# Output weights in three steps, and the side work of the output projections and of the first FFN products as timed events with four direct operands

## The chip, the core and the metric

The kernel runs on one core of a Trainium2 chip. The metric is the device time of one execution in microseconds (us). Times of runs are medians; the profile is of one further execution, traced by the hardware. Engines are named as the profile names them: PE (matrix products, PEld its weight loads), DVE (vector), ACT (scalar and activation), POOL, and SP, which here only issues DMAs. Each engine takes its instructions in one fixed order, and an instruction waits on semaphores for results of other engines or for DMAs. So an instruction that waits holds up everything behind it on its engine.

## What is computed

One layer of an encoder for two sequences of 1024 tokens with 1024 features (a prompt and a sample, which share the weights and are independent). Cut to what matters:

```python
def encoder_layer(x, ...):
    h = rms_norm(x, norm1)
    proj = h @ w_in                      # 1024 x 1792: q, k, v, gu, gv
    ...
    a = rms_norm(windowed_gqa(q, k, v, q_gain, k_gain, sink, rel_table), attn_out_gain)
    g = rms_norm(chunked_spatial_gating(gu, gv, v_gain, w_s, b_s), gmlp_out_gain)
    x = x + jnp.concatenate([a, g], axis=-1) @ w_o          # 1024 x 1024
    h2 = rms_norm(x, norm2)
    x = x + (jax.nn.silu(h2 @ w_gate) * (h2 @ w_up)) @ w_down   # 1024 x 2816, 2816 x 1024
```

The gating mixes the 128 positions of a chunk with one 128x128 matrix for each of 8 heads, and multiplies the result with `gelu(gu)`.

## The kernel before

The 2048 tokens are 16 tiles of 128 (`t` = 0 to 15; `s` = 0, 1 is the sequence). Every product is made with operands split in a high and a low half, so that one product takes three matmuls for each 128x128 block of weights. The work runs in stages.

**Attention and projections** end near 290 us. **The gating stage** follows, to about 455 us. It is the loop `for t in range(NT)` (L815). For each tile it makes two projections, `pgv` (`gm_pieces(t, 0)`) and `pgu` (`gm_pieces(t, 1)`), 8 k steps of 3 matmuls each. After every four tiles, at t = 5, 9 and 13, and once behind the loop, `gm_group` (L670) mixes the positions: for each head 3 matmuls into a `sg` tile in one of 4 PSUM buffers (L679 to L681), and two DVE operations (L684) that take it out again, into `u`. Beside this the output weights are made ready. `wo_step(k)` (L725) loads two blocks of `w_o`, multiplies them with their gain on ACT (L731), and makes two of six operands and their differences; `wo_step2(k)` makes the other four. Each operand costs an ACT cast (L113) and a DVE subtraction (L114). `WO_AT` and `WO2_AT` say behind which tile each stands.

**The output projections** run to 636 us: eight calls of `o_pair(n)` (L883), each for two tiles, `t` and `t + 4`. The product of 2x2 blocks is made with seven block products in place of eight, in the order `wa`, `wb`, `wa` again, `wc`, `wd`, `wc` again, `wd` again; a product is 12 matmuls. Their operands are sums of blocks of the transposed mixed activations: `o_turn(n + 1)` loads the `mix` tiles from DRAM, transposes them on PE (`pm`, 16 transposes) and makes operands `mo` on ACT and DVE. It is called in pair n behind product 1. Behind products 3 and 4, `o_h2` norms the tiles of the pair before: it transposes `xs` on PE (`ph`), scales by the norm weights on ACT into `hf` (L957), and stores blocks and block sums of the hidden state to DRAM (`t_d`). `o_norm` (L874) makes `xs` from the residual: a square with its sum on ACT (L878), a small power on DVE and POOL, and a multiplication on ACT (L880). `pair_hooks` (L1241) hangs loads of the FFN's operands on the last four pairs.

**The FFN** begins at 636.5 us with `matrix(n)` (L1127): gate and up products, each again seven block products of 12 matmuls (`pa`, `pb`, `pa`, `pc`, `pd`, `pc`, `pd`; L1079 to L1081). Their left operands `top` come back from `t_d` by `top_load` (`tr`, 512 KB each) and are split by `top_conv` on ACT (L997) and DVE (L998). In matrices 0 to 3, each step takes along `prep_op` (weights of a later matrix, L121 and L122) and `top_step` (loads and splits for the sample). Copies of the products out of PSUM, `ua` (L1197) and `ub` (L1208, L1212), stand on ACT among these. The down projection ends the program.

The order on each engine is not written out by hand. A scheduler takes the code order as the priority and, by its own costs, lets later instructions go first on an engine where it expects the earlier to be waiting. Buffers come from pools with tags (`XL`, `XN`, `S`, `L`), so a load waits until the last reader of its slot is done.

Of the kernel before, what the change touches and what calls it, by code (L numbers as in the profile page):

```python
# [16 lines left out]
P = 128  # L17
# [18 lines left out]
POS = ['', 't', '', '0', '1', '']  # L36
MIX_UP = 256.0
WO2_AT = (8, 10, 12, 14)
WO_AT = (6, 8, 10, 12)
# [12 lines left out]

TW = {
# [11 lines left out]
def kernel(  # L65
# [461 lines left out]
    def gm_pieces(t, z):  # L527
        nm_ = ("gv", "gu")[z]
        if z == 0:
            pxg[t] = k4("S", f"xg{t}", (P, 2, GW))  # L530
        elif t % GROUP:
            pxg[t] = grp[t // GROUP][0][t % GROUP // 2][:, t % 2, :]
# [4 lines left out]
        if z:  # L537
            dst = pxg[t] if t % GROUP else pxg[t][:, 1]
# [244 lines left out]
    def o_turn(n):  # L783
        xts, pms = [], []
        for t in pairs[n]:
            mx_ = k4("XL", f"mix{t}")
            load(mx_[:, 0:AW], mix_a[t])
            load(mx_[:, AW:D], mix_g[t])
            for z in range(2):
# [4 lines left out]
                pms.append(pt)  # L794
        for t in pairs[n]:
            xt = k4("XN", f"xr{t}")
            load(xt, xn[t])
            xts.append(xt)
        sc = h16(f"sc{n}", (P, 8, 4, P), F32)
        a11, a12, p21, a22 = pms  # L800
        a21, s1, s2, s3, s4 = (sc[:, i] for i in range(5))
        tl = [k4("S", f"mo{n}_{i}", (P, 2, 2, 4, P), F16) for i in range(4)]
        ops = [(tl[i // 2][:, i % 2, 0], tl[i // 2][:, i % 2, 1]) for i in range(7)]
        split16(*ops[0], a11)
# [3 lines left out]
        split16(*ops[5], a22)  # L808
        nc.vector.tensor_sub(s3, a11, a21)
# [4 lines left out]
        split16(*ops[4], s1)  # L814
        split16(*ops[6], s4)  # L815
        st_b[n] = (xts, sc, ops)

    for t in range(NT):
# [4 lines left out]
        if t % GROUP:  # L823
            if t == 1:
                gm_chain(0)
            if t % GROUP != 1 or t == 1:
                gm_chain(t)
        if t > GROUP and t % GROUP == 1:
            gm_group(t // GROUP - 1)
            gm_chain(t - 1)  # L830
            gm_chain(t)
        if t == NT - 1:
            o_turn(0)
        run(gm_pieces(t, 1))
# [9 lines left out]
        if t in WO2_AT:  # L844
            wo_step2(WO2_AT.index(t))

# [27 lines left out]
    def o_norm(t, xt):  # L874
# [8 lines left out]
    def o_pair(n, hooks=()):  # L883
        (x_t, x_u), sc, ops = st_b.pop(n)
# [7 lines left out]
        def half(j):  # L892
            if n >= 1:
                o_h2(pairs[n - 1][j])

        def turn():
            if n + 1 < len(pairs):
                o_turn(n + 1)

        def extra(i):  # L900
            for fn in hooks[i] if hooks else ():
                fn()
            for c in POS[i]:
                if c == "0":
                    half(0)
                elif c == "1":
                    half(1)
                else:
                    turn()

        pa = mm(f"wa{n}", [P, 512])
        o_product(ops, 0, pa, True, True)
        nc.scalar.copy(u2, pa)
        extra(0)
        pb = mm(f"wb{n}", [P, 512])
        o_product(ops, 1, pb, True, True)
        nc.vector.tensor_add(u2, pb, u2)
        extra(1)
        o_product(ops, 2, pa, False, True)
        done(x_t, 0, pa)  # L920
        extra(2)
        pc = mm(f"wc{n}", [P, 512])
        o_product(ops, 3, pc, True, True)
        nc.scalar.copy(p7, pc)
        extra(3)
        pd = mm(f"wd_{n}", [P, 512])
        o_product(ops, 4, pd, True, True)
        nc.scalar.copy(p5, pd)
        nc.vector.tensor_add(p7, p7, u2)
        extra(4)  # L930
        o_product(ops, 5, pc, False, True)
# [4 lines left out]
        o_norm(pairs[n][1], x_u)  # L936
        extra(5)
        o_product(ops, 6, pd, False, True)
        nc.vector.tensor_add(u2, pd, u2)
        done(x_t, 1, u2)  # L940
        o_norm(pairs[n][0], x_t)

    hfs = {}

    def o_h2(t):
        s, i = divmod(t, TS)
        half, q = divmod(i, 4)
        xs = st_b.pop(("x", t))
        hf = k4("L", f"hf{t}", (P, KD, P))
        for z in range(2):  # L950
# [4 lines left out]
            for j in range(4):  # L955
                k = z * 4 + j
                nc.scalar.mul(hf[:, k, :], pt[:, j, :], n2s[:, k : k + 1])  # L957
        cs = slice(q * P, (q + 1) * P)
        if half == 0:
            hfs[t] = hf  # L960
            store(t_d[s][B11][:, :, cs], hf[:, 0:4, :])
            store(t_d[s][B21][:, :, cs], hf[:, 4:8, :])
# [3 lines left out]
        store(t_d[s][B22][:, :, cs], b22)  # L966
# [6 lines left out]
        for op, src in ((T1, ta[:, 0]), (T2, ta[:, 1]), (T3, tb[:, 0]), (T4, tb[:, 1])):  # L973
            store(t_d[s][op][:, :, cs], src)

    B11, T2, B21, T3, T1, T4, B22 = range(7)
    tops = {}
    top16 = {}
# [3 lines left out]
    def top_load(s, i, z, tag="XL"):  # L982
        traw[s, i, z] = k4(tag, f"tr{s}_{i}_{z}", (P, 2, 512))
        load(traw[s, i, z], t_d[s][i][:, 2 * z : 2 * z + 2, :])

    def top_conv(s, i, z):
        if z == 0:
            if i < 4:
                if i % 2 == 0:
                    top16[s] = h16(f"top{s}_{i}", (P, 2, 2, 4, 512), F16)  # L990
                tops[s, i] = (top16[s][:, i % 2, 0], top16[s][:, i % 2, 1])
            else:
                tops[s, i] = tuple(k4("L", f"top{s}_{i}{c}", (P, 4, 512), F16) for c in "hl")
        hi, lo = tops[s, i]
        raw = traw.pop((s, i, z))
# [78 lines left out]
    def product(key, s, i, ps, first, last):  # L1074
        op = wops[key, i]
        th, tl = tops[s, i]
        for k in range(4):
# [19 lines left out]

    tq = [(i, z) for i in range(7) for z in range(2)]
    tn = [0]

    def top_step():
        k = tn[0]
        tn[0] += 1
        if k % 2 == 0:
            if k >= 4:
                top_conv(1, *tq[k // 2 - 2])
            top_load(1, *tq[k // 2])
        elif k == 2 * len(tq) - 1:
            top_conv(1, *tq[-2])
            top_conv(1, *tq[-1])  # L1110
# [405 lines left out]
```

## Time and profile before

| | us |
|---|---|
| median of 3 runs (1853.16 to 1853.8) | 1853.62 |
| the profiled execution | 1855.08 |
| its span in the trace | 1853.3 |
| PE busy (98% of the span) | 1815.3 |
| DVE busy (63%) | 1158.5 |
| ACT busy (54%) | 1009.5 |

The mean TensorE clock granted in that execution was 0.995. Read the table from the PE row: PE runs through nearly the whole span, so the time is PE's work plus PE's waits, and the waits are few. The view of the trace that lists them, by the instruction that waited and what released it, is where the prediction starts.

### The profile page before, as it was taken

The page shows a single profiled execution, that of the slowest core. Times are in us where ns is not written, and L with a number is a line of the kernel's source. Part 1 is how long each engine was busy: PE and PEld are TensorE (multiplying, and loading weights), DVE is VectorE, ACT ScalarE, POOL GpSimd, SP SyncE. Part 2 cuts the span into 40 slices and gives each one's busy share as a digit, 9 for nine tenths or more (in the row PEclk, how much of TensorE's full clock was granted, in tenths as well). Part 3 has the DMA queues.
Part 4 walks back from the last instruction along what each step waited for, and adds up shares of the span by engine and source line. Part 5 has one row for each costly group of instructions (what it writes and reads, how often), then busy time and mean ns, then how long its engine had stood idle before and what let it go on. Part 6 is the DMA issues. An engine that isn't in the chain of part 4 may idle for free.

```text
span 1853.3 us, 26039 instructions
## 1 busy us (share of the span) xinstructions
PE 1815.3 (98%) x9696; PEld 992.3 (54%) x9696; DVE 1158.5 (63%) x2183; ACT 1009.5 (54%) x1918; POOL 106.1 (6%) x139
## 2 busy tenths in 40 slices
PE   8999999999998999999999999999999999999999
PEld 7678767878554444444444444444444444444444
DVE  4988883665777896555545645645556956555761
ACT  6899997754666775444535534534444553333340
POOL 2122110111100000000000000000000000000000
PEclk9999999999999999999999999999999999999999
DMA  7799998432667874322313313313262764333641
GB/s 243 166 190 183 194 200 268 159 103 80 209 217 252 283 244 158 125 86 109 119 69 131 108 41 120 114 63 114 86 240 101 250 199 137 103 105 101 235 139 46
DMA packets 216027, 282.05 MB, mean 152 GB/s; under 512 B 103091, under 2 KB 137907, under 8 KB 215900
## 3 DMA queue, kind: packets, MB, share of 16 engines
q1 hardware_dynamic: 215724, 280.11, 49.4%
q8 instruction: 76, 1.25, 0.3%
q10 hardware_dynamic: 144, 0.26, 0.1%
q14 instruction: 51, 0.42, 0.1%
q0 software_dynamic: 32, 0.02, 0.0%
HBM read 177.04 MB, written 80.23 MB: 139 GB/s over the span
## 4 chain that ended last, share of the span: by engine, by line
PE 61%; DVE 2%; DMA 1%; ACT 1%; issue 0%; SPq 0%; POOL 0%; DVEq 0%
PE pd L1353 7%; PE pd L1355 7%; PE pd L1354 7%; PE pd L1079 4%; PE pd L1080 4%; PE pd L1081 4%; PE pa L1079 4%; PE pc L1079 4%; PE pa L1080 4%; PE pc L1080 4%; PE pc L1081 4%; PE pa L1081 4%; PE pb L1079 2%; PE pb L1080 2%; PE pb L1081 2%; DMA tr<-t_d 1%
## 5 line engine op out<-in xcount | busy, mean ns | idle before, releaser
L1355 PE MATMUL pd<-wop,a 128*128 128x512 f16 x616 | 233.5, 379 | 0.0
L1354 PE MATMUL pd<-wop,a 128*128 128x512 f16 x616 | 233.5, 379 | 0.0
L1353 PE MATMUL pd<-wop,a 128*128 128x512 f16 x616 | 233.5, 379 | 0.0
L1080 PEld LDWEIGHTS <-op 128*128 128x128 f16 x1232 | 120.6, 98 | 149.0 <-issue 7.4
L1081 PEld LDWEIGHTS <-op 128*128 128x128 f16 x1232 | 120.5, 98 | 146.5 <-issue 1.4
L1079 PEld LDWEIGHTS <-op 128*128 128x128 f16 x1232 | 122.3, 99 | 143.1 <-issue 0.3
L1079 PE MATMUL pa<-top,op 128*128 128x512 f16 x352 | 133.4, 379 | 0.5 <-ACT ua L1197 0.5
L1081 PE MATMUL pa<-top,op 128*128 128x512 f16 x352 | 133.4, 379 | 0.0
L1080 PE MATMUL pa<-top,op 128*128 128x512 f16 x352 | 133.4, 379 | 0.0
L121 ACT ACTIVATE wop<-wd,wdr_r 128x512 f16<-128x512 f32 x66 | 47.2, 720 | 150.9 <-PE pd L1355 147.4
L121 ACT ACTIVATE a<-as,asr_r 128x512 f16<-128x512 f32 x154 | 102.1, 710 | 33.6 <-DMA as<-act_d 15.4
L122 DVE SCALAR_TENSOR_TENSOR a<-as,asr_r,a 128x512 f16<-128x512 f32 x154 | 108.7, 746 | 6.3 <-ACT a L121 6.2
L1208 ACT COPY ub<-pc 128x512 f32<-128x512 f32 x44 | 25.7, 585 | 158.9 <-PE pc L1081 158.9
L122 DVE SCALAR_TENSOR_TENSOR wop<-wd,wdr_r,wop 128x512 f16<-128x512 f32 x66 | 49.2, 749 | 98.0 <-ACT wop L121 98.0
L1353 PEld LDWEIGHTS <-a 128*128 128x128 f16 x616 | 60.4, 98 | 72.5
L1355 PEld LDWEIGHTS <-a 128*128 128x128 f16 x616 | 60.3, 98 | 72.7
L1354 PEld LDWEIGHTS <-a 128*128 128x128 f16 x616 | 60.3, 98 | 72.6
L1022 ACT ACTIVATE junk_e<-g 128x1024 f32<-128x1024 f32 x44 | 46.3, 1053 | 70.4 <-DVE g L1192 70.4
L1214 DVE TENSOR_TENSOR ub<-ub,ua 128x512 f32<-128x512 f32 x44 | 30.4, 691 | 81.6 <-ACT ub L1208 79.2
L439 ACT ACTIVATE sc<-sc,mx 128x384 f32<-128x384 f32 (+1 forms) x128 | 74.3, 582 | 10.8 <-DVE mx L423 10.6
L1189 ACT ACTIVATE g<-g,rs 128x512 f32<-128x512 f32 x57 | 41.1, 721 | 62.5 <-DVE g L1224 35.5
L1079 PE MATMUL pd<-top_6h,op 128*128 128x512 f16 x176 | 66.7, 379 | 3.9 <-ACT ub L1212 3.7
(367 smaller groups left out, 4561.9 us busy)
## 6 DMA issues: line engine op xcount, KB each, us to landing
as<-act_d SPq DMA_DIRECT2D x77, 512.0 KB, 3.6
act_d<-g SPq DMA_DIRECT2D x66, 256.0 KB, 2.0
xs<-in_xT_dram SPq DMA_DIRECT2D x28, 512.0 KB, 4.4
tr<-t_d SPq DMA_DIRECT2D x28, 512.0 KB, 5.3
raw<-in_wg_dram SPq DMA_DIRECT2D x24, 512.0 KB, 4.0
raw<-in_wu_dram SPq DMA_DIRECT2D x24, 512.0 KB, 4.2
act_d<-sa SPq DMA_DIRECT2D x44, 256.0 KB, 2.5
act_d<-sb SPq DMA_DIRECT2D x44, 256.0 KB, 3.0
```

Source lines behind the costliest of these rows:

```text
L121: nc.scalar.mul(hi, src, gain)
L122: nc.vector.scalar_tensor_tensor(lo, src, gain, hi, ALU.mult, ALU.subtract)
L439: nc.scalar.activation(sc[:, v, :W], sc[:, v, :W], AF.Exp, bias=self.mn[:, h : h + 1], scale=-1.0, accum_out=self.sums[:, h : h + 1],)
L1022: nc.scalar.activation(junk_e[0], src, AF.Square, accum_out=acc)
L1079: nc.tensor.matmul(ps, op[:, 0, k, :], th[:, k, :], start=first and k == 0, stop=False, **more)
L1080: nc.tensor.matmul(ps, op[:, 0, k, :], tl[:, k, :], start=False, stop=False, **more)
L1081: nc.tensor.matmul(ps, op[:, 1, k, :], th[:, k, :], start=False, stop=last and k == 3, **more)
L1189: nc.scalar.activation(dst, src, AF.Silu, scale=iv)
L1214: nc.vector.tensor_add(p7, p7, u2)
L1353: nc.tensor.matmul(ps, a[:, 0, s, cs], wop[:, 0], start=first and n == 0, stop=False, **kw)
L1354: nc.tensor.matmul(ps, a[:, 0, s, cs], wop[:, 1], start=False, stop=False, **kw)
L1355: nc.tensor.matmul(ps, a[:, 1, s, cs], wop[:, 0], start=False, stop=end, **kw)
```

## The change

It has four parts. Line numbers in the changed code are some 5 to 40 higher.

1. The output weights come in three steps: `wo_load` (the two loads) behind tiles 5, 7, 10 and 11, `wo_step` behind 6, 8, 11 and 12 (before: 6, 8, 10, 12), `wo_step2` behind 7, 10, 11 and 13 (before: 8, 10, 12, 14). The gain multiplications may no longer be moved ahead of code that stands before them.
2. At t = 5, 9 and 13 the heads of the group and the k steps of `pgu` stand alternately in the code.
3. `o_turn` becomes `turn_a`, `turn_b`, `turn_c`; loads of `mix` and `xr`, `o_norm`, `o_h2`, the stores (`o_put`), the loads and splits of `top` and the first weights become events with a time in a table `DT`. The unit is one product; pair n begins at 7n, matrix n at 56 + 7n. Before each product `tick` runs what is due. `top_step`, `pair_hooks` and `POS` go.
4. Four operands of the prompt (`B11`, `T2`, `B21`, `T3`, the numbers 0 to 3) are split straight from `hf`, `ta` and `tb` into their `top` tiles (16 splits of 128x4x128, an ACT cast and a DVE subtraction each). Their 16 stores `t_d0_0` to `t_d0_3`, 8 loads `tr0_0` to `tr0_3` and 8 splits of 128x1024 go.

The issues on SP fall from 736 to 712, the DVE instructions go from 2184 to 2192, those on ACT from 1588 to 1596; PE has 9696 matmuls as before.

```diff
-WO2_AT = (8, 10, 12, 14)
-WO_AT = (6, 8, 10, 12)
+WO2_AT = (7, 10, 11, 13)
+WO_LD = (5, 7, 10, 11)
+WO_AT = (6, 8, 11, 12)
...
+DT = dict(
+    mx0=-13.949, mx1=-11.679, xr0=-11.199, xr1=-7.545, ta=-5.743, tb=-3.638, tc=1.886, nu=8.268, nt=8.797, h0=10.459,
+    p0=13, h1=14.83, p1=15.401, raw0=45.957, raw1=54.748, prep=52.704, preps=0.249, tl=57.369, tls=0.412, tk=58.051,
+    tks=0.597, ul=64.811, uls=0.974, uk=67.481, uks=0.956,
+)
...
+    def wo_load(k):
+        wraw[k] = [k4("XN", f"wr{j}", (P, 2, 512)) for j in (k, k + 4)]
+        for r, j in zip(wraw[k], (k, k + 4)):
+            load(r, w_o[j * P : (j + 1) * P, :].rearrange("p (z d) -> p z d", z=2))
+
     def wo_step(k):
-        r0 = k4("XN", f"wr{k}", (P, 2, 512))
-        r1 = k4("XN", f"wr{k + 4}", (P, 2, 512))
-        wraw[k] = (r0, r1)
+        r0, r1 = wraw[k]
         for r, j in ((r0, k), (r1, k + 4)):
-            load(r, w_o[j * P : (j + 1) * P, :].rearrange("p (z d) -> p z d", z=2))
-            nc.scalar.mul(r, r, wgain[:, j : j + 1])
+            tc.keep_in_program_order(nc.scalar.mul(r, r, wgain[:, j : j + 1]))
...
+        up = gm_pieces(t, 1)
         if t > GROUP and t % GROUP == 1:
-            gm_group(t // GROUP - 1)
+            group = gm_group_pieces(t // GROUP - 1)
+            while run(group, 1):
+                run(up, 1)
             gm_chain(t - 1)
             gm_chain(t)
...
-        run(gm_pieces(t, 1))
+        run(up)
...
+    def o_put(t):
+        s, i = divmod(t, TS)
+        half, q = divmod(i, 4)
+        hf = h2s.pop(t)
+        puts.append(t)
         cs = slice(q * P, (q + 1) * P)
+
+        def put(op, src):
+            if s == 0 and op < 4:
+                if op % 2 == 0 and (s, op) not in tops:
+                    top_pair(s, op)
+                hi, lo = tops[s, op]
+                split16(hi[:, :, cs], lo[:, :, cs], src)
+            else:
+                store(t_d[s][op][:, :, cs], src)
...
+        def mul(i, ps, first, last):
+            if n < 6:
+                tick(56 + 7 * n + i)
+            product(key, s, i, ps, first, last)
...
+    def tick(time):
+        while side and side[0][0] <= time:
+            _, _, fn, args = side.pop(0)
+            fn(*args)
+
+    for n, pair in enumerate(pairs):
+        T = 7 * n
+        for j, t in enumerate(pair):
+            if n:
+                do(T + DT[f"mx{j}"], mix_load, t)
+                do(T + DT[f"xr{j}"], xr_load, t)
+            do(T + DT["nt" if j == 0 else "nu"], o_norm, t)
+            do(T + DT[f"h{j}"], o_h2, t)
+            do(T + DT[f"p{j}"], o_put, t)
+        if n:
+            do(T + DT["ta"], turn_a, n)
+            do(T + DT["tb"], turn_b, n)
+            do(T + DT["tc"], turn_c, n)
+    do(DT["raw0"], load_raw, (0, 0), "S")
+    do(DT["raw1"], load_raw, (0, 1))
+    for i in range(7):
+        do(DT["prep"] + i * DT["preps"], prep_op, (0, 0), i)
+    for k in range(6):
+        do(DT["tl"] + k * DT["tls"], top_load, 0, 4 + k // 2, k % 2)
+        do(DT["tk"] + k * DT["tks"], top_conv, 0, 4 + k // 2, k % 2)
+    for k in range(14):
+        do(DT["ul"] + k * DT["uls"], top_load, 1, k // 2, k % 2)
+        do(DT["uk"] + k * DT["uks"], top_conv, 1, k // 2, k % 2)
+    side.sort(key=lambda e: e[:2])
     for n in range(len(pairs)):
-        o_pair(n, pair_hooks(n))
...
+        o_pair(n)
+    tick(56)
```

How this moves instructions is seen at three places. The first is DVE at t = 9, ahead of the first two operations that take `sg` out (`wo..l` are low halves of output weight operands, `wr` raw output weights, `xl` the low half of a later tile's input). Before:

```order
L114 TENSOR_TENSOR wo0l<-wr_5438,wo0h 128x512
L735 TENSOR_TENSOR wr_5438<-wr_5438 128x512
L114 TENSOR_TENSOR wo4l<-wr_5438,wo4h 128x512
L736 TENSOR_TENSOR wr_5438<-wr_5439,wr_5438 128x512
L114 TENSOR_TENSOR wo2l<-wr_5439,wo2h 128x512
L737 TENSOR_TENSOR wr_5439<-wr_5439,wr_5438 128x512
L114 TENSOR_TENSOR wo3l<-wr_5438,wo3h 128x512
L684 SCALAR_TENSOR_TENSOR u_0_4858<-sg_0_5220,cst,u_0_4858 128x2x64
L684 SCALAR_TENSOR_TENSOR u_1_4859<-sg_0_5220,cst,u_1_4859 128x2x64
L684 SCALAR_TENSOR_TENSOR u_0_4858<-sg_1_5226,cst,u_0_4858 128x2x64
```

After:

```order
L196 TENSOR_TENSOR xl_5191<-xs_5187,xh_5189 128x1024
L119 TENSOR_TENSOR wo1l<-wr_5112,wo1h 128x512
L119 TENSOR_TENSOR wo5l<-wr_5112,wo5h 128x512
L688 SCALAR_TENSOR_TENSOR u_0_4883<-sg_0_5220,cst,u_0_4883 128x2x64
L688 SCALAR_TENSOR_TENSOR u_1_4884<-sg_0_5220,cst,u_1_4884 128x2x64
L688 SCALAR_TENSOR_TENSOR u_0_4883<-sg_1_5230,cst,u_0_4883 128x2x64
L688 SCALAR_TENSOR_TENSOR u_1_4884<-sg_1_5230,cst,u_1_4884 128x2x64
L688 SCALAR_TENSOR_TENSOR u_0_4883<-sg_2_5239,cst,u_0_4883 128x2x64
L688 SCALAR_TENSOR_TENSOR u_1_4884<-sg_2_5239,cst,u_1_4884 128x2x64
```

Of the third pair of weight blocks, seven operations stood right ahead of the first `u<-sg`; now none of that pair does, and the last weight operations there are of the pair before it, behind which `xl` also stands. On PE, behind each `sg` (3 matmuls) there are now 3 matmuls of `pgu`. At t = 13, the order after has seven operations of the last two weight blocks ahead of the first `u<-sg` of that group, where before there were two `xl` and two `vl`.

The second place is SP in the output projections, at the loads of `mix10` and `mix14`, which PE transposes for pair 6 (`x1_d` are stores of the residual, `tr0` loads of FFN operands, `xr` loads of the residual). Before:

```order
L875 DMA x1_d12_138<-xr12_6778 128x1024
L984 DMA tr0_1_0_7191<-t_d0_1_143 128x1024
L875 DMA x1_d8_134<-xr8_6776 128x1024
L797 DMA xr13_7001<-in_xn_dram 128x1024
L787 DMA mix10_7207<-mix_a10_104 128x512
L788 DMA mix10_7207<-mix_g10_120 128x512
L787 DMA mix14_7220<-mix_a14_108 128x512
L788 DMA mix14_7220<-mix_g14_124 128x512
L797 DMA xr10_7233<-in_xn_dram 128x1024
L984 DMA tr0_1_1_7290<-t_d0_1_143 128x1024
```

After:

```order
L793 DMA mix10_6930<-mix_a10_104 128x512
L798 DMA xr7_6460<-in_xn_dram 128x1024
L794 DMA mix10_6930<-mix_g10_120 128x512
L798 DMA xr8_6596<-in_xn_dram 128x1024
L911 DMA x1_d7_133<-xr7_6460 128x1024
L911 DMA x1_d3_129<-xr3_6367 128x1024
L991 DMA t_d0_6_148<-hf6_6933 512x1x128
L991 DMA t_d0_4_146<-ta6_7008 512x1x128
L793 DMA mix14_7047<-mix_a14_108 128x512
L794 DMA mix14_7047<-mix_g14_124 128x512
L991 DMA t_d0_5_147<-tb6_7009 512x1x128
```

The loads of `mix10` and `mix14` stood behind the stores of tiles 12 and 8, the residual of pair 4, with `tr0` loads on both sides; now `mix10` stands ahead of, and `mix14` behind, the stores of tiles 7 and 3, the residual of pair 3, and no `tr0` load is near.

The third place is ACT in matrix 2 of the FFN (names `.._1_0_0`), ahead of the copy `ua1_0_0`, for which PE's third product of that matrix waits (`junk_e` are squares with their sum; `tr1` loaded operands of the sample). Before:

```order
L121 ACTIVATE op1_0_6_8209<-st1_0_8147,es_er_5997 128x512
L997 CAST top1_2_8190<-tr1_3_0_8193 128x1024
L1022 ACTIVATE junk_e_8214,asum0_6101<-g0_0_1_7931 128x1024
L997 CAST top1_2_8190<-tr1_3_1_8254 128x1024
L1022 ACTIVATE junk_e_8214,asum0_6101<-g0_0_0_7930 128x1024
L1197 COPY ua1_0_0_8232<-pa1_0_0_8234 128x512
```

After:

```order
L1036 CAST top1_0_8143<-tr1_1_0_8124 128x1024
L1036 CAST top1_0_8143<-tr1_1_1_8146 128x1024
L1061 ACTIVATE junk_e_8187,asum0_6101<-g0_0_1_7786 128x1024
L1036 CAST top1_2_8247<-tr1_2_0_8166 128x1024
L1061 ACTIVATE junk_e_8187,asum0_6101<-g0_0_0_7785 128x1024
L1226 COPY ua1_0_0_8205<-pa1_0_0_8207 128x512
```

The copy still stands behind the square of `g0_0_0`, but the splits ahead of it are of the operands 1 and 2 now, where they were of operand 3. On PE, between `pb1_0_0` and that third product, 7 of the 12 matmuls of `pc1_0_0` stand now; before, all 12 did.

More of the change, by code (lines that the diff above doesn't have):

```diff
@@ L808, in o_turn, with turn_b @@
         split16(*ops[5], a22)
+        st_b[n][2].extend((0, 2, 5))
+    def turn_b(n):
+        sc, ops, done = st_b[n]
+        a11, a12, p21, a22 = pms.pop(n)
+        a21, s1, s2, s3, s4 = (sc[:, i] for i in range(5))
         nc.vector.tensor_sub(s3, a11, a21)
@@ L832 @@
         if t == NT - 1:
-            o_turn(0)
-        run(gm_pieces(t, 1))
+            for q in pairs[0]:
+                mix_load(q)
+            turn_a(0)
+            for q in pairs[0]:
+                xr_load(q)
+            turn_b(0)
+            turn_c(0)
+        run(up)
         if 1 <= t < 5:
@@ L881, in o_norm, with o_pair, product @@
         st_b["x", t] = xs
-    def o_pair(n, hooks=()):
-        (x_t, x_u), sc, ops = st_b.pop(n)
+    def o_pair(n):
+        def product(i, ps, first, last):
+            tick(7 * n + i)
+            assert i in st_b[n][2]
+            o_product(st_b[n][1], i, ps, first, last)
+        sc = st_b[n][0]
+        x_t, x_u = (xrs.pop(t) for t in pairs[n])
         flat = [sc[:, i].rearrange("p a b -> p (a b)") for i in range(8)]
@@ L935, in o_pair @@
         done(x_u, 1, p7)
[L936 to L938 removed]
+        x1s[pairs[n][1]] = x_u
+        product(6, pd, False, True)
         nc.vector.tensor_add(u2, pd, u2)
         done(x_t, 1, u2)
[L941 to L943 removed]
+        x1s[pairs[n][0]] = x_t
+        del st_b[n]
+    x1s = {}
+    hfs, h2s, puts = {}, {}, []
     def o_h2(t):
[L946 to L947 removed]
         xs = st_b.pop(("x", t))
@@ L983, in top_load, with top_pair @@
         traw[s, i, z] = k4(tag, f"tr{s}_{i}_{z}", (P, 2, 512))
+        assert s == 0 or len(puts) == NT
         load(traw[s, i, z], t_d[s][i][:, 2 * z : 2 * z + 2, :])
+    def top_pair(s, i):
+        pair = h16(f"top{s}_{i}", (P, 2, 2, 4, 512), F16)
+        for j in range(2):
+            tops[s, i + j] = (pair[:, j, 0], pair[:, j, 1])
     def top_conv(s, i, z):
@@ L1147, in prep @@
                     soon((1, 0), i)
-                top_step()
                 return
```

164 lines of the change are left out of this document (54 added, 110 removed).

## The prediction

> **What bounds the kernel now.** I read the busy shares first.
>
> ```profile
> PE 1815.3 (98%) x9696; PEld 992.3 (54%) x9696; DVE 1158.5 (63%) x2183; ACT 1009.5 (54%) x1918; POOL 106.1 (6%) x139
> ```
>
> PE is busy for 98% of the span and the number of matmuls stays, so a change can win only PE's idle time and slow matmuls, and lose only by new waits of PE. The second view, PE's waits, lists most of that idle time (line, releaser, total, times, longest).
>
> ```profile
> PE sg L679 <- DVE u L684: 5.4, 3, 4.5
> PE pm L793 <- DMA mix<-mix_a: 4.3, 2, 2.2
> PE pd L1079 <- ACT ub L1212: 3.7, 2, 1.9
> PE ph L954 <- ACT xs L880: 2.3, 1, 2.3
> PE wa L870 <- ACT sc L913: 1.1, 2, 0.7
> PE pd L1080 <- DVE top_6l L998: 0.9, 1, 0.9
> PE pa L1079 <- ACT ua L1197: 0.5, 1, 0.5
> PE pc L1079 <- ACT ub L1208: 0.4, 1, 0.4
> PE pd L1079 <- ACT top_6h L997: 0.2, 1, 0.2
> ```
>
> All nine lie in code that the change touches, and they sum to 18.8 us. The waits of the attention stage, which it leaves alone, are not quoted. The third view, the span in windows (wall time, busy time and instructions of PE, PEld, DVE, ACT and POOL, then the granted clock, the share of the DMA engines and GB/s), says where they lie.
>
> ```profile
> 350.00:400.00 50.00, 45.52 (x201) 38.08 (x200) 36.15 (x76) 35.04 (x63) 6.56 (x8) 0.93 0.44 149
> 400.00:450.00 50.00, 50.00 (x242) 42.10 (x241) 17.93 (x47) 18.48 (x40) 4.39 (x8) 1.00 0.22 74
> 550.00:600.00 50.00, 45.50 (x244) 24.57 (x242) 36.58 (x59) 33.76 (x73) 4.00 (x5) 1.00 0.77 249
> 600.00:650.00 50.00, 46.78 (x234) 24.73 (x235) 40.01 (x62) 40.05 (x90) 3.65 (x5) 0.97 0.87 280
> 650.00:700.00 50.00, 46.14 (x211) 20.51 (x210) 45.49 (x63) 35.65 (x51) 0.00 (x0) 1.00 0.76 245
> ```
>
> The first row holds the group at t = 9, the second tiles behind it without any PE idle, the next two the last output projections and matrix 0, the last the next matrices. In two rows the granted clock is below 1. Asked in windows that fit the dips, PE alone:
>
> ```profile
> 374.70:381.50 6.80, 5.81 (x20) 0.50 0.25 77
> 641.00:644.40 3.40, 1.11 (x9) 1.00 0.95 354
> 644.40:647.80 3.40, 3.40 (x15) 0.50 0.75 235
> 579.86:586.66 6.80, 6.80 (x45) 1.00 0.85 308
> ```
>
> After the waits at 375 and 643 us PE ran at half clock: 5.81 us busy at 0.50 did 2.9 us of work, so 2.9 us were lost, and 3.40 / 2 = 1.7 us at the second. After the wait of 2.2 us for `mix`, which ends where the last window begins, it did not. So what hangs on these waits is 18.8 + 2.9 + 1.7 = 23.4 us.
>
> The Trainium skill, "TensorE: Matmul & The Clock Gate", section "HAM oscillation — how this bites in real kernels", gives as the rule that PE should have no idle gap above about 3.4 us. By that rule the 2.3 us wait would have cost its own length only and the sum would be 1.7 us smaller; the row of 0.50 behind it says otherwise, so the measurement decides, and a short new wait may carry a dip.
>
> **Part by part.** *Weights and heads at t = 9.* The operations of DVE ahead of the wait, and the matmul that waited:
>
> ```profile
> 368.92 0.69 DVE L114 TENSOR_TENSOR wo0l<-wr,wo0h 128x512 f16<-128x512 f32 x1 [1.93 <-ACT wo0h L113]
> ...
> 374.94 2.15 DVE L684 SCALAR_TENSOR_TENSOR u<-sg,cst,u 128x128 f32<-128x128 f32 x8
> ```
> ```profile
> 375.69 0.55 PE L679 MATMUL sg<-vh,ws_hi 128*128 128x256 f32 x1 [4.48 <-DVE u L684]
> ```
>
> Seven operations of output weights, with waits for ACT among them, filled DVE from 368.9 to 375 us; four `sg` filled the four buffers and the fifth had to wait. In the order after, none of these seven is ahead of the `u` operations, so the 4.48 us and the 2.9 us of half clock go: -7.4. The two matters cover each other: even if DVE came late, three matmuls of `pgu` now lie behind each `sg`. A product of 12 such matmuls takes 2.59 us (rows below), so that is 0.65 us for each of the four heads, 2.6 us in all. The weight work itself does not vanish: it moves to t = 10 to 13, where the row of 400 to 450 us leaves DVE and ACT busy less than 19 of 50 us, and to t = 13, where seven operations now stand ahead of `u`. The same delay there, less 2.6 us, would cost 1.9 us; nothing at the other end, if ACT's casts come earlier. I take 0.5, near nothing, since by the code order the last weights' loads stand two tiles ahead. The 0.9 us of the last group (5.4 - 4.48) stays: its order is as before.
>
> *Output projections.* The waits for `mix` (4.3) and for `wa` (1.1) sum to 5.4 us. Both `mix` loads of each pair are now issued a pair earlier, on SP ahead of what held them, so -4.3. The copy out of `wa` moves up ACT's order, ahead of the squares: -1.1. The steady pair is the cover for everything else that was moved here, so it has to be walked, first PE, then ACT:
>
> ```profile
> 507.24 1.91 PE L793 MATMUL pm<-ident,mix 128*128 128x128 f32 x16
> 508.98 0.38 PE L870 MATMUL wa<-wo2h,mo 128*128 128x512 f16 x1
> ...
> 514.16 1.04 PE L954 MATMUL ph<-ident,xs 128*128 128x128 f32 x8
> 515.04 0.38 PE L870 MATMUL wd<-wo4h,mo 128*128 128x512 f16 x1
> ...
> 517.63 1.04 PE L954 MATMUL ph<-ident,xs 128*128 128x128 f32 x8
> ```
>
> ```profile
> 507.75 1.15 ACT L880 ACTIVATE xs<-xr,a_r 128x1024 f32<-128x1024 f32 x1 [0.45 <-POOL a_r L156]
> 511.81 1.66 ACT L113 CAST mo<-sc 128x512 f16<-128x512 f32 x3
> 518.31 2.18 ACT L957 ACTIVATE hf<-ph,n2s 128x128 f32<-128x128 f32 x8
> ```
>
> From start to start, a tile's `ph` takes 0.88 us, a product 2.59 (515.04 to 517.63), the `pm` of a pair 1.74. In the order after, a pair's ACT has between the first `ph` and the second `xs` product: `hf` (2.18), two squares (2.1; one of this shape takes 1.06 in a row below), two casts and a copy (1.5), `xs` (1.05), three casts (1.5, at about 0.5 each behind one another), `xs` (1.15). That is 9.5 us, from about 3.0 us after the pair's start (behind one product and half of the `ph` transposes) to 12.5. PE needs this `xs` for the next `ph` after four products, one `ph` and the `pm` transposes: 4 x 2.59 + 0.88 + 1.74 = 13.0. The slack is 0.5 us. Bounds are nothing, and 1 us in each of 6 pairs; I take 0.5 us in all, near the walked slack. The 16 splits of direct operands, 0.5 us of ACT and at most 0.69 us of DVE each, are in that walk; what they replace, splits of 128x1024, is below.
>
> *The FFN's start.* The wait of `ph` at matrix 0 goes, since the last `ph` are spread over matrix 0 and their `xs` are made earlier: -2.3 - 1.7. The waits of matrices 0 to 3 (3.7 + 0.9 + 0.5 + 0.4 + 0.2 = 5.7) are for ACT and DVE, which split what is loaded for `top`:
>
> ```profile
> 686.38 1.06 ACT L1022 ACTIVATE junk_e<-g 128x1024 f32<-128x1024 f32 x1 [3.71 <-DVE g L1192]
> 690.12 0.56 ACT L1197 COPY ua<-pa 128x512 f32<-128x512 f32 x1
> ```
> ```profile
> 683.14 1.22 DVE L998 TENSOR_TENSOR top<-tr,top 128x1024 f16<-128x1024 f32 x1
> 684.27 0.69 DVE L1221 TENSOR_TENSOR ub<-ub 128x512 f32<-128x512 f32 x1
> 684.88 0.75 DVE L122 SCALAR_TENSOR_TENSOR op<-st,es_er,op 128x512 f16<-128x512 f32 x1
> 685.54 0.75 DVE L1192 SCALAR_TENSOR_TENSOR g<-ub,es_er,g 128x512 f32<-128x512 f32 x1
> ```
> ```profile
> tr<-t_d SPq DMA_DIRECT2D x28, 512.0 KB, 5.3
> ```
>
> These change but do not all go. In matrix 0 a copy `ub` now stands behind a split: between nothing and 1.9 us, the longest `ub` wait of before; I take 0.65, since a split (1.0) and no load is ahead of it. `top_6h` keeps its 0.2. In matrix 3 the `ub` copy behind the loads of `top_6` lies between the same ends; I take 0.6, since these loads are issued earlier.
>
> Matrix 2 can be walked. There the copy `ua1_0_0` stands behind the splits of `tr1_1_1` and `tr1_2_0`, whose loads wait for a slot until DVE has split `tr1_0_0` and `tr1_0_1`. One after another DVE's operations take 1.13 us (split), 0.61 (add) and 0.66 (`op`). With the matrix's start as zero, the fifth product of matrix 1 ends at -5.2; copy (0.6), add, `op` and split give -2.2; `op`, add and split 0.2. With 5.3 us of landing the second load is there at 5.5; split (1.0), square (1.2) and copy (0.6) end at 8.2 or 8.3. PE asks after two products and 7 matmuls, at 6.7: a wait of 1.5 us. If the load takes 4 us, it is 0.4 (then DVE's result for the square comes last), if 6.5, 2.7. New and left: 0.65 + 0.2 + 0.6 + 1.5 = 2.95.
>
> **Sum.** -7.4 + 0.5 - 5.4 + 0.5 - 4.0 - 5.7 + 2.95 = -18.55 us. The profiled execution took 1855.08 us, so 1836.5; it stands 1.46 us above the median 1853.62, which gives 1835.1, say 1835.0.
>
> **Rivals.** (A) *All waits go*: -23.4 and the 0.9 of the last group back, 1831.1. For it speaks that many loads are issued earlier; against it that DVE is busy 45.5 of 50 us from 650 to 700. (B) *ACT comes late in the pairs and at matrix 2*: 1 us in six pairs (+5.5 on my 0.5), 2.7 us with a half-clock dip at matrix 2 (+1.2 + 1.7): 1843.5. For it speaks the slack of 0.5 us. (C) *The change doesn't do what it says at the weights*: the wait of t = 9 turns up at t = 13 with its half clock, 4.5 + 2.9 where I have 0.5: 1842.0. The seven operations speak for it, the `pgu` matmuls behind each `sg` against it. (D) *Slower*: the second `xs` of a pair is 2.5 us late in ACT's order, so PE waits 2.0 us and falls to half clock for a window, 1.7 us; six pairs cost 22.2 us, which is 1856.8 with 0.5 taken off. It decides from an `xs` that ends past 15 us of the pair's start instead of 12.5; against it speaks that ACT is busy 33.8 of 50 us there, and that no wait of that kind stood in pairs 1 to 5.
>
> **How the numbers follow.** My forecast has 0.55, A 0.13, B 0.15, C 0.08, B and C together, 1850.4, 0.05, D 0.04. The range reaches from A to past B, 1830 to 1845, and leaves the last two out. About 0.2% (3.7 us) is what a measurement of this kernel can tell from no change: faster by more 0.91, within 0.05, slower by more 0.04.
>
> **What would show it.** In the trace after: no `sg` wait at about 370 us and a granted clock of 1 there; no `pm` wait; in each pair no `ph` wait on `xs`, or one of under 0.5 us; at matrix 2 a `pa` wait on `ua` of 0.4 to 2.7 us; waits of about 3 us in matrices 0 to 3 in place of 5.7. Wrong would be: a `sg` wait at t = 13, `ph` waits in every pair, or a clock of 0.5 behind a wait that I have as short.

## The result and the profile after

The changed kernel takes 1835.32 us, the median of 4 runs (1832.81 to 1836.35), beside 1853.71 us before (4 runs): a ratio of 0.9888, 95% interval 0.9874 to 0.9902. The forecast was 1835.0 in a range of 1830 to 1845. The profiled execution took 1836.35 us, its span is 1834.5. First the busy shares of the changed kernel, and below them its view of PE's waits (line, releaser, total, times, longest; lines are those of the changed code):

```profile
PE 1809.8 (99%) x9696; PEld 988.6 (54%) x9696; DVE 1161.2 (63%) x2191; ACT 1005.3 (55%) x1926; POOL 104.4 (6%) x139
```
```profile
PE po L489 <- DMA pT<-ph: 6.1, 4, 3.2
...
PE pa L1119 <- ACT ua L1226: 2.0, 1, 2.0
PE pc L1119 <- ACT ub L1237: 1.5, 2, 1.0
PE sg L683 <- DVE u L688: 0.9, 2, 0.6
```

Of the nine kinds of wait that the prediction listed, with 18.8 us, these three are left in the code that was changed, with 4.4 us. No `pm`, `wa`, `ph` or `top_6` is among them, and `sg` has the 0.9 us of the last group only. (`po` is in the attention stage, which the change leaves alone; it comes up again at the end.) The same windows as before, then the one dip that is new:

```profile
350.00:400.00 50.00, 50.00 (x233) 41.78 (x233) 31.43 (x67) 29.37 (x61) 4.94 (x9) 1.00 0.43 148
550.00:600.00 50.00, 50.00 (x269) 27.16 (x267) 41.04 (x69) 35.57 (x86) 3.40 (x4) 1.00 0.64 218
600.00:650.00 50.00, 49.53 (x249) 24.84 (x248) 40.28 (x61) 40.26 (x85) 3.55 (x4) 1.00 0.72 235
650.00:700.00 50.00, 47.00 (x211) 20.80 (x209) 44.22 (x59) 31.84 (x44) 0.00 (x0) 0.97 0.75 248
668.50:671.90 3.40, 1.41 (x8) 1.00 0.87 320
671.90:675.30 3.40, 3.40 (x10) 0.50 1.00 368
```

Where PE was busy 45.5 of 50 us at t = 9 and in the last output projections, it is busy without a break. The loss that remains lies in matrices 0 to 3, and the greater part at matrix 2: a wait of 2.0 us and, behind it, 3.4 us at half clock.

The change of the profiled executions is 1855.08 - 1836.35 = 18.73 us. The terms as measured: t = 9 gave 7.4, `mix` and `wa` 5.4, `ph` at matrix 0 with its dip 4.0, and in matrices 0 to 3 5.7 went, 0.5 + 2.0 + 1.0 of waits and 1.7 of dip came. That makes 17.3. Of the other 1.4 us, the attention stage had one half clock (1.7) less and 1.2 us more of `po` wait in this execution; the rest, 0.9 us, isn't placed.

### The profile page after: what moved, and what is told of

Its sections match the earlier page's. It is cut to its first block, busy times and chain, and to the rows that moved or that the text cites. A ratio compares the mean times of both kernels' runs of the same rounds, so it can differ in the third digit from the quotient of the medians.

```text
span 1834.5 us, 26027 instructions
## 1 busy us (share of the span) xinstructions
PE 1809.8 (99%) x9696; PEld 988.6 (54%) x9696; DVE 1161.2 (63%) x2191; ACT 1005.3 (55%) x1926; POOL 104.4 (6%) x139
## 4 chain that ended last, share of the span: by engine, by line
PE 91%; DVE 3%; DMA 2%; ACT 2%; issue 1%; POOL 0%; SPq 0%; ACTq 0%; POOLq 0%; DVEq 0%
PE pd L1382 7%; PE pd L1383 7%; PE pd L1381 7%; PE pa L1119 4%; PE pa L1121 4%; PE pa L1120 4%; PE pd L1119 4%; PE pd L1121 4%; PE pd L1120 4%; PE pc L1120 4%; PE pc L1121 4%; PE pc L1119 4%; PE pb L1119 2%; PE pq L226 2%; PE pb L1120 2%; PE pb L1121 2%
## 5 line engine op out<-in xcount | busy, mean ns | idle before, releaser
L1119 PE MATMUL pc<-top_5h,op 128*128 128x512 f16 x176 | 66.7, 379 | 1.5 <-ACT ub L1237 1.5
```

The costliest lines, as they stand in the source:

```text
L1119: nc.tensor.matmul(ps, op[:, 0, k, :], th[:, k, :], start=first and k == 0, stop=False, **more)
```

## The experiments

All ratios are to runs of the kernel before on the same chip. Between chips the kernel before ran from 1853.7 to 1856.0 us, so kernels are compared by their ratio or within a set.

**Each part of the gating stage undone.** Heads ahead of `pgu` again:

```diff
-            while run(group, 1):
-                run(up, 1)
+            run(group)
```

> The changed kernel, with the heads of each group ahead of pgu again and not alternating with it; the weights stay in three steps. My theory: the seven weight operations ahead of the first u were the cause of the 4.5 us wait at t = 9, and they stay away there, so the sg wait at t = 9 is under 1 us and the clock there is 1; at t = 13, where seven operations stand ahead of u, the 2.6 us cover is gone and a wait of 1.9 to 4.5 us shows. In all 1 to 6 us above the changed kernel. Rival: the alternation is what removed the wait at t = 9; then about 4.5 us and a half clock return there, 7 us or more above the changed kernel.

Measured: ratio 0.9885 (0.9870 to 0.9900), as the changed kernel. There is no `sg` wait at t = 9, and one of 1.4 us at t = 13:

```profile
420.51 0.36 PE L683 MATMUL sg<-vh,ws_hi 128*128 128x256 f32 x1 [1.43 <-DVE u L688]
```

So the dates of the weights suffice at t = 9; at t = 13, where they put the same work, it is the alternation that hides it. The wait there was smaller than I had it, 1.4 for 1.9 to 4.5, and of the 1 to 6 us that I expected in the time nothing shows.

The weights at their old tiles, loads inside the first step, heads alternating:

```diff
-WO2_AT = (7, 10, 11, 13)
-WO_LD = (5, 7, 10, 11)
-WO_AT = (6, 8, 11, 12)
+WO2_AT = (8, 10, 12, 14)
+WO_AT = (6, 8, 10, 12)
...
-        r0, r1 = wraw[k]
+        r0 = k4("XN", f"wr{k}", (P, 2, 512))
+        r1 = k4("XN", f"wr{k + 4}", (P, 2, 512))
+        wraw[k] = (r0, r1)
         for r, j in ((r0, k), (r1, k + 4)):
-            tc.keep_in_program_order(nc.scalar.mul(r, r, wgain[:, j : j + 1]))
+            load(r, w_o[j * P : (j + 1) * P, :].rearrange("p (z d) -> p z d", z=2))
+            nc.scalar.mul(r, r, wgain[:, j : j + 1])
```

> The changed kernel, with the weights in two steps at the old tiles (loads inside the first step, 6, 8, 10, 12 and 8, 10, 12, 14) and free to move; the heads still alternate with pgu. Five operations of the third weight blocks stand ahead of the first u at t = 9 again. My theory: they make u late by what they did, 4.5 us, of which the pgu matmuls cover 2.6: an sg wait of 0 to 1.9 us at t = 9, without half clock, so 0 to 2 us above the changed kernel. Rival: the dates are what counts, and the wait is as before, 4.5 us and 2.9 us of half clock, 7.4 us above it.

Measured: ratio 0.9902 (0.9886 to 0.9919). The profile has the wait at t = 9 at 2.4 us, without half clock:

```profile
PE sg L682 <- DVE u L687: 3.3, 3, 2.4
```

The alternation alone leaves 2.4 of 4.5 us. Its cover is a little more than the difference: with both parts undone (the next version) the wait begins 1.6 us after the start of the first `sg` and ends 6.0 us after it; here it begins at 4.4 and ends at 6.8. So the cover is 2.8 us, near the 2.6 that I had, and `u` came 0.7 us later. The wait lies between the numbers of the two theories, as a cover and not the cause would leave it.

Both undone together:

> The changed kernel, with both parts in the gating stage undone: weights in two steps at the old tiles, heads ahead of pgu. My theory: the term is the whole of what these two parts give, and it doesn't depend on the rest: the sg wait of 4.5 us at t = 9 and 2.9 us of half clock return, no other wait changes by over 1 us: 7.4 us above the changed kernel. Rival: the two single undoings, 0 and 2.4 us of wait at t = 9, show that the rest of the change has eased DVE there too; then under 5 us.

Measured: 1840.12 us, ratio 0.9917 (0.9893 to 0.9941), which is some 5 us above the changed kernel's 0.9888, between the two theories. The waits, and three windows beside the wait:

```profile
PE sg L682 <- DVE u L687: 5.3, 3, 4.5
```
```profile
371.10:374.51 3.41, 0.19 (x1) 0.99 0.00 0
374.51:377.90 3.39, 3.39 (x13) 0.50 0.53 155
377.90:381.31 3.41, 3.41 (x18) 1.00 0.00 0
```

The 4.5 us are all back, so nothing else in the change eases that place. But the half clock took one window here, 1.7 us, where the kernel before had two, 2.9 us. The term was 6.2 in this execution and 7.4 in that.

**The gating parts alone.** The kernel before, with the weights in three steps and the alternation (and the place of `pgu`'s result chosen as in the changed kernel):

> The kernel before, with the weights in three steps and the alternation of heads and pgu alone. My theory: of the change's gain just the term of 7.4 us appears: 1846.3 us, no sg wait over 1 us, and the waits for mix, ph and the FFN's start stay as before (16.3 us with a dip). Rival: the faster gating stage shifts what follows and part of it comes back as longer waits for mix, 1848 us or more.

Measured: 1848.44 us, ratio 0.9961 (0.9948 to 0.9974): 7.2 us by the ratio (4.8 to 9.6). Most of the other waits stay as they were:

```profile
PE pm L795 <- DMA mix<-mix_a: 4.4, 2, 2.2
PE pd L1086 <- ACT ub L1219: 3.8, 2, 1.9
PE ph L961 <- ACT xs L887: 2.3, 1, 2.3
PE pd L1086 <- ACT top_6h L1004: 1.3, 1, 1.3
...
PE sg L679 <- DVE u L684: 1.1, 3, 0.6
```

The term stands by itself: the waits for `mix`, which the rival had growing, stay as they were (4.4 us for 4.3). One other wait is longer in this execution: `top_6h` has 1.3 us where the kernel before had 0.2, so that the waits of the later stages sum to 15.0 us and not to 13.4. Whether that comes from the earlier gating stage isn't shown.

**The direct operands undone**, so that they go to DRAM and back:

```diff
-            if s == 0 and op < 4:
+            if False:
...
+    for k in range(8):
+        do(36.6 + 2.2 * k, top_load, 0, k // 2, k % 2)
+        do(39.1 + 2.2 * k, top_conv, 0, k // 2, k % 2)
```

> The changed kernel, with the four direct operands written to DRAM and loaded and split again as before (16 stores, 8 loads, 8 splits of 128x1024 at dates between products 36 and 55). My theory: the wait for mix went since its loads are issued earlier, so no pm wait over 0.5 us returns, and the 8 splits find room on ACT and DVE: 0 to 2 us above the changed kernel. Rival: the loads tr0 held the slots and the DMA engines; with them back, two pm waits of about 2 us return, 4 us or more above the changed kernel.

Measured: ratio 0.9911 (0.9896 to 0.9926), 1839.32 us.

```profile
PE ph L971 <- ACT xs L916: 2.4, 2, 2.1
PE pa L1119 <- ACT ua L1226: 1.7, 2, 1.5
PE pc L1119 <- ACT ub L1237: 1.3, 2, 0.8
```

No `pm` wait came back, so it is the order of the `mix` loads and not the number of loads that freed PE there. But the 8 splits did not find room. The last pair's ACT shows why (start, time, and what it waited for):

```profile
604.92 1.04 ACT L1036 CAST top<-tr 128x1024 f16<-128x1024 f32 x1 [2.52 <-DMA tr<-t_d]
607.60 1.05 ACT L1036 CAST top<-tr 128x1024 f16<-128x1024 f32 x1 [1.64 <-DMA tr<-t_d]
608.55 0.58 ACT L936 COPY sc<-wa 128x512 f32<-128x512 f32 x1
...
615.64 0.70 ACT L126 ACTIVATE op<-ss,es_er 128x512 f16<-128x512 f32 x1
616.26 0.70 ACT L126 ACTIVATE op<-raw,es_er 128x512 f16<-128x512 f32 x1
616.87 1.13 ACT L916 ACTIVATE xs<-xr,a_r 128x1024 f32<-128x1024 f32 x1
```

Splits that wait for loads, and weight work (`op`), stand ahead of the last `xs`; the thin slack of the pair is used up, PE waits 2.1 us for `xs` at 618 us, and a half clock of 1.7 us follows. The direct operands are worth about 4 us, with dates that I chose for their loads.

**The last transposes where they were.** The `ph` of the last pair and its stores due at the start of matrix 0. Their `xs` (`o_norm`) are due just before it too, which the expectation, with everything else as changed, doesn't say:

```diff
-            do(T + DT["nt" if j == 0 else "nu"], o_norm, t)
-            do(T + DT[f"h{j}"], o_h2, t)
-            do(T + DT[f"p{j}"], o_put, t)
+            do(min(T + DT["nt" if j == 0 else "nu"], 55.99 + 0.001 * (1 - j)), o_norm, t)
+            do(56 + 0.01 * j if n == 7 else T + DT[f"h{j}"], o_h2, t)
+            do(56.1 + 0.01 * j if n == 7 else T + DT[f"p{j}"], o_put, t)
...
-    tick(56)
+    tick(56.5)
```

> The changed kernel, with the four ph of the last pair and its stores due at the start of matrix 0, where the kernel before had them; everything else as changed. The scheduler sets three of them behind 10 matmuls of the second product, as before. My theory: PE asks for xs 4.7 us after the matrix's start, and ACT has it only about 7 to 10 us after it (in the changed kernel the last xs ends 10.5 us after it): a ph wait of 2.3 to 4 us with a half clock of 1.7, so 4 to 6 us above the changed kernel. Rival: with early loads and direct operands ACT is free at that point and xs is there in time: no ph wait, within 1 us.

Measured: 1841.09 us, ratio 0.9916 (0.9895 to 0.9937), about the 4 to 6 us of my theory, but by another way:

```profile
PE pc L1119 <- ACT top_5h L1036: 3.2, 1, 3.2
PE pa L1119 <- ACT ua L1226: 1.2, 1, 1.2
...
PE ph L971 <- ACT xs L916: 0.8, 1, 0.8
```
```profile
649.00 1.04 ACT L1036 CAST top_5h<-tr 128x1024 f16<-128x1024 f32 x1 [3.25 <-DMA tr<-t_d]
```

With its `xs` due first, ACT has the last one 5.7 us after the start of matrix 0 (629.2 for a start at 623.6), and the `ph` wait is 0.8 us; this speaks for the rival, though with an `xs` that was moved up. What is late then is a load: ACT was idle for 3.25 us ahead of the split of `top_5` for which PE waited 3.2 us, with a half clock behind it. The 24 `hf` operations come almost in one run, their 12 stores follow from 631 to 642 us, and SP issued this load behind the last of them, at 642.4 us, where the changed kernel issues it at 632.2. So the spread gives PE's later question for `xs`, and by SP's order it also keeps the stores out of this load's way; that second part wasn't tried by itself.

**The wait of matrix 2.** The changed kernel was run again beside three versions.

> The changed kernel once more, beside the next three on one chip. My theory of the clock: the half clock begins only at one grid of windows of 3.41 us for each execution, and only behind a window with 1.95 us or more of PE idle time. So the wait at matrix 2 is again about 2 us, and it brings a half clock of 3.4 us only if one window holds nearly all of it; PE's idle time in the window ahead of each half clock is over 1.95 us, and no window with over 2.0 us goes without. Rival: a wait of about 2 us is enough wherever it lies; then the half clock follows it here again.

Measured: 1835.05 us (1833.16 to 1837.00), ratio 0.9893 (0.9878 to 0.9908). The wait at matrix 2 was 1.4 us, and no half clock followed. It tells the theories of the clock apart only with the other profiles; see the last section.

The two squares held behind the fourth product of matrix 2:

```diff
-        nc.scalar.activation(junk_e[0], src, AF.Square, accum_out=acc)
+        i_ = nc.scalar.activation(junk_e[0], src, AF.Square, accum_out=acc)
+        if held:
+            tc.keep_in_program_order(i_)
...
+                if n == 1:
+                    do(73.5, square_sum, *args, True)
+                    side.sort(key=lambda e: e[:2])
+                else:
+                    square_sum(*args)
```

> The changed kernel, with the two squares of the prompt's first products held behind the fourth product of matrix 2, so that the copy ua1_0_0 has them no more ahead of it on ACT. The loads of raw1_1 come earlier by this too. My theory: the load of tr1_2_0, which waits for a slot, is what is late; without the squares the copy ends 1.2 us earlier and still behind the split of tr1_2_0: the wait falls from 2.0 to about 0.8 us, no half clock, 1 to 3 us faster than the changed kernel. Rival: the square, which waits for DVE, sets the end; then the wait falls to nothing.

Measured: 1835.45 us, ratio 0.9896 (0.9881 to 0.9910). The `pa` wait is gone, more than I expected, and nothing is gained. (The load ahead of `ua` landed after 4.4 us here; by the rule that the next section finds, that would have left a wait of 0.5 us with the squares in place, so this run is no measure of what they cost there.) The wait that came, and ACT's order:

```profile
PE pc L1121 <- ACT ub L1239: 3.5, 3, 2.3
```
```profile
667.75 1.05 ACT L1036 CAST top<-tr 128x1024 f16<-128x1024 f32 x1 [2.13 <-DMA tr<-t_d]
668.71 0.58 ACT L1228 COPY ua<-pa 128x512 f32<-128x512 f32 x1
672.23 1.05 ACT L1036 CAST top<-tr 128x1024 f16<-128x1024 f32 x1 [2.94 <-DMA tr<-t_d]
675.20 1.04 ACT L1036 CAST top<-tr 128x1024 f16<-128x1024 f32 x1 [1.93 <-DMA tr<-t_d]
676.15 0.68 ACT L1215 ACTIVATE g<-pa,es_er 128x512 f32<-128x512 f32 x1
676.73 1.05 ACT L1061 ACTIVATE junk_e<-g 128x1024 f32<-128x1024 f32 x1
...
677.77 0.57 ACT L1239 COPY ub<-pc 128x512 f32<-128x512 f32 x1
```

The copy that PE needs next, `ub`, now stands behind two splits that wait 2.9 and 1.9 us for their loads, and behind one of the two squares, which the new date puts right ahead of it. The wait moved by one copy, from 2.0 to 2.3 us, of which about 1 us is the square. So it is the loads ahead of the copies, as my theory had it, and at this copy the moved square as well.

So in the next version the splits stand behind the copies too:

```diff
-        nc.scalar.copy(hi[:, zs, :], raw)
+        i_ = nc.scalar.copy(hi[:, zs, :], raw)
+        if s == 1 and (i, z) >= (1, 1):
+            tc.keep_in_program_order(i_)
...
-        do(DT["uk"] + k * DT["uks"], top_conv, 1, k // 2, k % 2)
+        do(DT["uk"] + k * DT["uks"] + (2.2 if k >= 12 else 0), top_conv, 1, k // 2, k % 2)
```

> As square_later, with the splits of the sample from tr1_1_1 on held in code order, behind the copy ua1_0_0, and the last two (tr1_6) two products later, behind the copies ub of matrix 3. My theory: nothing that waits for a late load is left ahead of these copies, so the waits at matrix 2 (2.0) and of ub in matrix 3 (1.0) go, with the half clock behind the first: 3 to 5 us faster than the changed kernel, about 1831. Rival: DVE is then the bound at that place (44 of 50 us busy) and a wait of 1 us or more for DVE takes their place; under 2 us faster.

Measured: 1834.60 us (1832.44 to 1836.96), ratio 0.9889 (0.9872 to 0.9905), so not the 3 to 5 us. The two waits are gone, and one of 1.1 us is new. The gain has the size of the rival, under 2 us, but PE waits there for ACT, where the rival had DVE; what stands right ahead of the copy is again a square that was held back, 1.05 us from 680.8 on, and no load is waited for there. PE's waits:

```profile
PE pd L1123 <- ACT ub L1245: 1.1, 1, 1.1
PE pc L1123 <- ACT ub L1241: 0.5, 1, 0.5
```

Beside the first profile of the changed kernel that is 3.6 us less in the changed stages (2.0 + 1.5 + 1.7 of dip for 1.6), beside the second 1.1 us. The profiled execution gave it back in the attention stage, where `po` waited 4.5 us with two windows at half clock.

Last, the first gate of matrix 0, with ACT's table load of 1.28 us in front of it, behind the copy `ub`:

```diff
-        out_(g0[:, 0], pa)
+        if n:
+            out_(g0[:, 0], pa)
         prep(2)
...
         nc.scalar.copy(p7, pc)
+        if n == 0:
+            tc.keep_in_program_order(nc.scalar.activation(g0[:, 0], pa, AF.Silu, scale=iv))
```

> As copy_first, with the first gate of matrix 0, which has the load of ACT's table in front of it (1.28 us), behind the copy ub of the same matrix. My theory: the wait of 0.47 us for that copy goes and nothing else moves: 0.5 us faster than copy_first, which is less than the runs can tell, so the profile decides: no pc wait on ub at matrix 0. Rival: the gate, now later, holds the splits of top0_5 behind it, and a wait for these of 0.5 us or more appears.

> The fastest of the versions so far, once more on this chip. My theory: it is faster than the changed kernel by the waits of matrices 2 and 3 that it doesn't have, 1.2 us in the profile, and by the half clock that these give the changed kernel in some executions, so 1.5 to 3.5 us: a ratio to the kernel before of 0.987 to 0.989. Rival: its 1831.4 was owed to the attention stage, whose waits differ from run to run by 4 us; then 1834 to 1836.

Measured: 1831.43 us (1830.43 to 1832.46), ratio 0.9873 (0.9859 to 0.9888), and in the second set 1831.81 us, 0.9870 (0.9849 to 0.9891). It is the fastest version, 3.6 us under the changed kernel beside it, with no run of either in the other's range.

```profile
PE po L489 <- DMA pT<-ph: 5.1, 5, 2.7
PE pd L1123 <- ACT ub L1248: 1.1, 1, 1.1
...
PE pc L1123 <- ACT top_5h L1036: 0.4, 1, 0.4
```

The gate itself gave nothing: its rival held, a wait of 0.4 for `top_5h` has taken the place of 0.5 for `ub`. Why this version is 3 us under copy_first, with nearly the same waits but for that one, is open. The profiles lay it in the attention stage, whose code is the same in both; that the time came again on another chip speaks against chance alone.

## Why the prediction was right

*The bound.* PE's work stayed and PE's waits set the time; 18.73 us between the profiled executions stand for 18.55 in the sum. That they agree to 0.2 us is in part luck: the code that was changed gave 17.3 us, since the two small losses of 0.5 didn't come and matrices 0 to 3 lost 2.25 us more than forecast, and 1.4 us came from outside the terms.

*t = 9: -7.4, and +0.5 at t = 13.* Right, and shown from three sides: both parts undone bring the 4.5 us back, alone they give 7.2 us. The two parts don't do the same: the dates empty DVE's queue at t = 9, the alternation covers what the dates put at t = 13 (1.4 us without it, nothing with it). The 2.9 us of half clock was a size of one execution; another gave 1.7.

*Output projections: -5.4, +0.5.* All of the 5.4 went, and no new wait came. The walked slack of 0.5 us is in the trace, where the second `xs` of a pair ends at 506.84 and its `ph` starts at 507.24:

```profile
505.60 1.24 ACT L916 ACTIVATE xs<-xr,a_r 128x1024 f32<-128x1024 f32 x1
...
507.24 1.04 PE L971 MATMUL ph<-ident,xs 128*128 128x128 f32 x8
```

That the wait for `mix` went by the order of its loads is shown by the version with the loads `tr0` back, which has no `pm` wait. That version also shows what the prediction passed over: the direct operands had no term of their own, and they keep about 4 us away. In the last pairs the slack is so thin that a split behind a late load puts PE in wait, the mechanism of rivals B and D at one place.

*Matrix 0: -4.0.* The size was right, but of the reason only one half. I wrote that the last `xs` are made earlier. They are not: the last ends 10.5 us after the start of matrix 0 (632.8 for a start at 622.2), where in the kernel before `ph` had it after 7.2. It is only that PE asks later, 11.2 us after the start, since `ph` is spread; so the part of the term that was to come from earlier `xs` is nothing.

*Matrices 0 to 3: -5.7, +2.95.* Here the new waits were mis-sized. They came to 0.5 (0.65 + 0.2 forecast), 2.0 (1.5) and 1.0 (0.6), and to a half clock of 1.7 that I had in rival B and not in the forecast. The walk of matrix 2 named the right instructions:

```profile
664.10 1.04 ACT L1036 CAST top<-tr 128x1024 f16<-128x1024 f32 x1 [4.21 <-DMA tr<-t_d]
665.05 1.05 ACT L1061 ACTIVATE junk_e<-g 128x1024 f32<-128x1024 f32 x1
...
668.15 1.04 ACT L1036 CAST top<-tr 128x1024 f16<-128x1024 f32 x1 [1.96 <-DMA tr<-t_d]
669.11 1.05 ACT L1061 ACTIVATE junk_e<-g 128x1024 f32<-128x1024 f32 x1
...
670.16 0.56 ACT L1226 COPY ua<-pa 128x512 f32<-128x512 f32 x1
```

With the start of the matrix at 661.9, the second split begins at 6.2 (5.5 forecast) and the copy ends at 8.8 (8.2 to 8.3). The difference is the landing of one load, which took 5.9 us and not 5.3. Six profiles have this order: the two of the changed kernel, those with one part or both of the gating stage undone, and the one with the direct operands undone. In all six the load is issued 0.3 us after the start of the matrix, and the wait is the time that it takes to land less 3.88 us. In order of size, 4.66, 5.03, 5.31, 5.38, 5.72 and 5.87 us of landing gave waits of 0.78, 1.15, 1.43, 1.50, 1.84 and 1.99 us. So the load sets this wait, as the walk had it, and all are within the bounds of 0.4 and 2.7. (With the last `ph` at the start of matrix 0 another order stands there; a square that waits for DVE comes last, and the wait is 1.2.)

The rivals: A is too good, since copies still stand behind loads; of B only the half clock at matrix 2 came, and only in one of the two profiles of the changed kernel; C didn't come, as the alternation covers t = 13; D didn't come, as the second `xs` of a pair was there at least 0.4 us before its `ph` in every pair.

## What to carry to other kernels

Where an engine takes its work in order and PE waits for a small copy on it, look at what stands ahead of that copy: an operation that waits for a load costs PE the load's lateness, however short the operation is, and what is moved from ahead of one copy stands ahead of the next. A walk of one steady period on the engine with the thinnest slack, made from durations in the trace, was right to 0.1 us; it is worth making before anything is put there. Work that must be done somewhere is best put beside matmuls that don't need it, rather than only ahead of those that do.

## What the runs showed of the hardware

The half clock of PE keeps to a grid. In the 8 of the 13 profiles that have more than one half-clock stretch, those at the program's two ends left out, the stretches begin at multiples of 3.41 us from one another. With that grid laid through each profile, and PE's idle time summed in each window, 24 of the 25 stretches follow a window with 1.99 us of idle time or more. No window at full clock with 1.92 or less brings one, but for one in the attention stage of the kernel before (1.16). Three stretches last two windows; the first of the two had 0.95 to 1.01 us of idle time itself, that of the others 0.37 or less. Two waits, of 2.2 and 1.9 us, from the kernel with the gating parts alone, show it:

```profile
567.70:571.10 3.40, 1.32 (x7) 1.00 0.97 344
571.10:574.50 3.40, 3.24 (x12) 0.50 0.87 350
670.10:673.51 3.41, 1.51 (x8) 1.00 0.44 142
```

PE was busy 1.32 us in the first window and fell to half clock in the next; it was busy 1.51 us in the third and did not. A wait of 2.2 us for `mix` brought a half clock in this kernel and none in the kernel before, where the grid divided it. The plainest case is one that all 13 profiles have from the same code: near 48 us the matmuls `pj` wait 2.35 us for `v`. In 6 profiles a half clock follows, with 2.00 us or more of idle time in one window; in 7 none does, and there the grid divides the wait so that no window has over 1.89. So a window with under 1.9 us of idle time cost more than that only once here, a wait of 2 to 3.4 us costs 1.7 us more if the grid leaves 2 us of it in one window, and one of 4.5 us cost 1.7 or 2.9 more. The Trainium skill, "TensorE: Matmul & The Clock Gate", section "What's actually happening", says that the activity window is 4096 cycles, about 3.4 us, and runs free. The grid of 3.41 us agrees, while the bound of 3.4 us for a gap, which the prediction took from the same page, is too long for these traces. No run set the grid's place on purpose; it fell otherwise from execution to execution.

The attention stage, the same code in all, waited for `po` between 4.5 and 7.0 us in the 13 profiles, with none, one or two windows of half clock behind the longest of these waits. That alone makes up to 5 us between two profiles (4.9 us and no half clock in one, 7.0 us and 2.9 us lost to half clock in another), more than the last versions differ by.
